# Gate and up projections of three feed-forward groups by seven half-size products instead of eight, in an encoder trunk on one core

## The chip, the cores and the metric

The kernel runs on one core of one Trainium2 chip. The metric is the device time of one execution in microseconds, as the median of several runs. The profile is one further execution, recorded by the hardware profiler; its span is counted from its first to its last instruction.

## The reference

The reference is a two-layer encoder trunk on 256 tokens of width 1024, all in float32. Cut to what matters here:

```python
def swiglu(h, w_gate, w_up, w_down):
    return (jax.nn.silu(h @ w_gate) * (h @ w_up)) @ w_down

for l in range(2):
    x = x + 0.5 * swiglu(rms_norm(x, ffn1_norm[l]), ffn1_w_gate[l], ffn1_w_up[l], ffn1_w_down[l])
    ...   # windowed attention with sinks, differential attention, one output projection
    x = x + 0.5 * swiglu(rms_norm(x, ffn2_norm[l]), ffn2_w_gate[l], ffn2_w_up[l], ffn2_w_down[l])
return rms_norm(x, final_norm)
```

So there are four feed-forward stages. In each, `w_gate` and `w_up` are 1024 x 2816 and `w_down` is 2816 x 1024.

## The kernel before

**Split products.** Every float32 weight tile is cut into a high and a low part. ScalarE (ACT) writes the high part (`whi`, a CAST of the loaded tile `raw`), VectorE (DVE) writes the rest (`wlo`, a TENSOR_TENSOR subtract of `raw` and `whi`). The normalised input x and the hidden values are cut in the same way, into two halves of a tile `s`. A product is then three TensorE (PE) matmuls: x high with w high, x low with w high, x high with w low. Tokens come in two tiles of 128, which are the stationary operand; the weights stream through as 512 columns.

**Steps.** One weight tile is a step: 128 partitions x 4 k-blocks x 512 columns, 1 MB. The SyncE queue (SP) loads it into one of 6 `raw` buffers, `emit_split` (line 167) cuts it in two halves of 128 x 1024 into one of 3 `whi` and one of 3 `wlo` buffers, and PE uses it in 24 matmuls (4 k-blocks, 2 token tiles, 3 matmuls each). A hidden group is 512 columns of gate and of up: four steps for gate and up (two k-halves each) and two steps for the down projection of the group before (`down`, line 623). The 2816 columns are groups 0 to 4 and a last half-wide one (lines 642 to 666). Between the first and the second gate step PE turns the hidden values of the group before with 8 transposes (`turn`, line 609), ACT and DVE cut the result into `hT`.

**What sets the order.** The order of every engine's queue is the order in which the program emits instructions (`keep_in_program_order`; inside the attention a scheduler may move them). `weights()` (line 219) returns the parts of the next step and first calls `ahead`, which emits the cut of the step after the next (`LOOK` is 2), a preparation step (`prep`) one step further, and the loads of up to 8 steps further while a `raw` buffer is free. Each queue works in order: an instruction that waits holds up all that is behind it. PSUM has 8 banks, 4 of which hold the down projection's sums through the whole stage.

**Code that lies idle.** The kernel already has `seven` (line 115), `make_sums` (line 304), `prod` (line 565) and `by_seven` (line 575). They are used for the groups named in `SEVEN` (line 31), which is empty, so that they never run. Also in the file and unchanged are `quarter` and `summed` (lines 333 and 340), which hand `prod` a quarter of x or one of the sums.

Of the kernel before, what the change touches and what calls it, by code (L numbers as in the profile page):

```python
# [27 lines left out]
LOOK, AHEAD = 2, 8  # L28
N_RAW, N_HI, N_LO = 6, 3, 3
N_S4 = 16  # L30
SEVEN = ()


@with_exitstack
def trunk(ctx: ExitStack, tc: tile.TileContext, x, n1, g1, u1, d1, nm, w_in, sink,
# [31 lines left out]
    def nm_(s):  # L67
        uid[0] += 1
        return f"{s}_{uid[0]}"

    def bank():
        return ps.tile([P, 512], F32, tag="ps", bufs=8, name=nm_("ps"))

    def halves(b):
        return b.rearrange("p (a n) -> p a n", a=2)

    def blk(dt=F32R):
        return s4.tile([P, 2, 512], dt, tag="s4", name=nm_("s4"))

    def tmp(tag="tmp", bufs=5, shape=(P, 2, 256), dt=F32):  # L80
        return tp.tile(list(shape), dt, tag=tag, bufs=bufs, name=nm_(tag))
# [137 lines left out]
    def weights(look=LOOK):  # L219
        i = at["use"]  # L220
        at["use"] += 1
        if i > 1:
            ahead(i + look)
        return loaded.pop(i)

    for l in range(DEPTH):
        def ffn_specs(wg, wu, wd):
# [3 lines left out]
            for g in range(1, NGRP):  # L231
                downs = [down(g - 1, h) for h in range(2)]
                if g in SEVEN:
                    specs.extend(seven(wg[l], wu[l], g * 512, downs))
# [38 lines left out]
    class Norm:  # L273
# [30 lines left out]
        def make_sums(self):  # L304

            self.sm = []

            def part(b, t):

                vs = [f(self.xs[2 * b + i]) for i in range(2)]  # L310
                return [[v[:, :, c + t * P:c + (t + 1) * P] for v in vs] for c in (0, S)]

            def make(x, y, op, rest):
                v = tmp().rearrange("p a (c s) -> p (a c) s", c=2)
                for i in range(2):
                    vi = v[:, 2 * i:2 * i + 2]
                    dve.tensor_tensor(vi, x[i], y[i], op=op)
                    for z, o in rest:
                        dve.tensor_tensor(vi, vi, z[i], op=o)
                sm = blk().rearrange("p a (c s) -> p (a c) s", c=2)  # L320
                act.copy(sm[:, :, 0:P], v)
                dve.tensor_tensor(sm[:, :, P:S], v, f(sm[:, :, 0:P]), op=ALU.subtract)
                self.sm.append(sm)
                return [v[:, 0:2], v[:, 2:4]]

            add, sub = ALU.add, ALU.subtract
            (t0h, t0l), (t1h, t1l), (b0h, b0l), (b1h, b1l) = [part(b, t) for b in range(2) for t in range(2)]
            s1 = make(b1h, t1h, sub, [(b1l, add), (t1l, sub)])
            s2 = make(s1, t0h, add, [(t0l, add)])
            make(t1h, t0h, sub, [(t1l, add), (t0l, sub)])  # L330
            make(b0h, s2, sub, [(b0l, add)])

        def quarter(self, t, b):

# [48 lines left out]
    norm = Norm(0)  # L383
# [86 lines left out]
    def tokens(accs, xs, w, k0, ks=range(4), first=0, last=KC - 1, order=None):  # L470

        hi, lo = w
        for k, t in (order or [(k, t) for k in ks for t in range(2)]):
            kk = k0 + k
            xv = xs[kk // 2][:, kk % 2]
            xh, xl = xv[:, t * P:(t + 1) * P], xv[:, S + t * P:S + (t + 1) * P]
            pe.matmul(accs[t], lhsT=xh, rhs=hi[:, k], start=kk == first, stop=False)
            pe.matmul(accs[t], lhsT=xl, rhs=hi[:, k], start=False, stop=False)
            pe.matmul(accs[t], lhsT=xh, rhs=lo[:, k], start=False, stop=kk == (last if isinstance(last, int) else last[t]))
# [63 lines left out]
    def ffn(norm, aside=None, before=None, final=False):  # L543
        def silu(out_, acc, t):
            act.activation(out_, acc, AF.Silu, scale=norm.r[:, t:t + 1])
            return out_

        def gate(gs):
            g = []
            for t in range(2):  # L550
                n = gs[t].shape[1]
                g.append(silu(tmp().rearrange("p a n -> p (a n)")[:, :n], gs[t], t))
            return g

        def up(h, acc, g, t):
            n = acc.shape[1]
            dve.scalar_tensor_tensor(h[:, t, :n], in0=acc, scalar=norm.hr[:, t:t + 1], in1=g, op0=ALU.mult, op1=ALU.mult)

        def hidden(g, us):
            h = blk(F32)  # L560
            for t in range(2):
                up(h, us[t], g[t], t)
            return h

        def prod(xo):
            hi, lo = weights()
            acc = bank()
            for k in range(4):
                xh, xl = xo(k)
                pe.matmul(acc, lhsT=xh, rhs=hi[:, k], start=k == 0, stop=False)  # L570
                pe.matmul(acc, lhsT=xl, rhs=hi[:, k], start=False, stop=False)
                pe.matmul(acc, lhsT=xh, rhs=lo[:, k], start=False, stop=k == 3)
            return acc

        def by_seven(h, g):

            flat = lambda: tmp().rearrange("p a n -> p (a n)")

            def put(o, x, y, op):
                dve.tensor_tensor(o, x, y, op=op)  # L580
                return o

            p1 = prod(norm.quarter(0, 0))
            m1 = flat()
            act.copy(m1, p1)
            p7 = prod(norm.summed(2))
            hT = turn(h, 2)
            p6 = prod(norm.summed(1))
            u2 = put(flat(), p6, m1, ALU.subtract)
            u3 = put(flat(), p7, u2, ALU.add)  # L590
            down(hT, g - 1, 0, weights())
            h = blk(F32)
            p2 = prod(norm.quarter(0, 1))
            g0 = put(m1, p2, m1, ALU.add)
            silu(g0, g0, 0)
            p4 = prod(norm.quarter(1, 1))
            g1 = put(flat(), p4, u3, ALU.subtract)
            silu(g1, g1, 1)
            p5 = prod(norm.summed(0))
            put(u3, u3, p5, ALU.subtract)  # L600
            put(u2, u2, p5, ALU.subtract)
            up(h, u3, g1, 1)
            p3 = prod(norm.summed(3))
            put(u2, u2, p3, ALU.add)
            up(h, u2, g0, 0)
            down(hT, g - 1, 1, weights())
            return h

        def turn(hs, n):
            out_ = []  # L610
            for i in range(n):
                sl = halves(bank())
                for c in range(2):
                    for t in range(2):
                        pe.transpose(sl[:, c, t * P:(t + 1) * P], hs[:, t, (2 * i + c) * P:(2 * i + c + 1) * P], ident)
                hb = blk()
                split(hb, sl)
                out_.append(hb)
            return out_

        accs = [[bank(), bank()] for _ in range(2)]

        def down(hT, g, h, w):
            tokens(accs[h], [None] * (2 * g) + hT, w, 4 * g, last=(FC - 1, G4 - 1) if final and h else FC - 1)


        gs, us = [bank(), bank()], [bank(), bank()]
        if before is None:
            before = norm.late
        before(0)  # L630
        ws = (weights(), weights(LOOK - 1))
        for k in (0, 2):
            if k:
                before(1)
            for sl, w in zip((gs, us), ws):
                tokens(sl, norm.xs, w, 0, (k, k + 1))
        before(2)
        tokens(gs, norm.xs, weights(), 4)
        g = gate(gs)
        tokens(us, norm.xs, weights(), 4)  # L640
        h = hidden(g, us)
        for n in range(1, NGRP):
            if n + 1 == min(SEVEN, default=0):
                norm.make_sums()
            if n == 3 and aside is not None:
                aside()
            if n in SEVEN:
                h = by_seven(h, n)
                continue
            gs = [bank(), bank()]  # L650
            tokens(gs, norm.xs, weights(), 0)
            hT = turn(h, 2)
            tokens(gs, norm.xs, weights(), 4)
            g = gate(gs)
            us = [bank(), bank()]
            for k0 in (0, 4):
                tokens(us, norm.xs, weights(), k0)
            h = hidden(g, us)
            for hh in range(2):
                down(hT, n - 1, hh, weights())  # L660

        gu = [bank(), bank()]
        tokens(gu, norm.xs, weights(), 0)
        hT = turn(h, 2)
        tokens(gu, norm.xs, weights(), 4)
        h = hidden(gate([b[:, 0:256] for b in gu]), [b[:, 256:512] for b in gu])
        return accs, hT, lambda: turn(h, 1)
# [278 lines left out]
    for l in range(DEPTH):  # L946
# [7 lines left out]
        if not final:  # L954
            norm = Norm((l + 1) * 8)
# [71 lines left out]
```

## Time and profile before

| what | value |
|---|---|
| median of 3 runs | 964.58 us (964.55 to 965.61) |
| the profiled execution, its own time | 964.2 us |
| its span | 962.4 us |
| TensorE clock granted, mean | 0.997 of full |
| PE busy | 951.3 us, 99% of the span |
| weight loads of PE (PEld) busy | 807.9 us, 84% |
| DVE busy | 557.4 us, 58% |
| ACT busy | 478.2 us, 50% |
| POOL busy | 20.1 us, 2% |
| read from HBM | 167.54 MB, 175 GB/s over the span |

Each engine is one row of the profile. Matmuls overlap each other, so the durations of single matmuls add up to more than the busy time, and the pitch between them has to be read from start times. A row of the timeline is start, time from the first start to the last end, engine, operation, output and inputs, count, and in brackets how long the engine had stood idle before and who ended that.

### The profile page before, as it was taken

The numbers are of one execution on the slowest core, as the hardware profiler recorded it, in microseconds if no ns is written. First come the engines' busy times: TensorE is split into PE (matmuls) and PEld (weight loads), VectorE is DVE, ScalarE is ACT, GpSimd is POOL, SyncE is SP. The second block draws the span as 40 slices with busy tenths as digits, with TensorE's granted clock in tenths as the row PEclk, the third lists the DMA queues.
The fourth block names the chain that finished last, engine by engine and source line by source line (L and its number), as shares of the span: only waits on it lengthen the run. The fifth ranks groups of instructions, "written<-read, shape, count | busy, mean of one in ns | idle before, by whom it ended". The sixth has DMA issues, their size and how long they took to land.

```text
span 962.4 us, 12393 instructions
## 1 busy us (share of the span) xinstructions
PE 951.3 (99%) x4940; PEld 807.9 (84%) x4940; DVE 557.4 (58%) x854; ACT 478.2 (50%) x781; POOL 20.1 (2%) x49
## 2 busy tenths in 40 slices
PE   8999999999999999999999999999999999999997
PEld 6888888899888888888888888888999888888886
DVE  5555545579756555545665445556796665445453
ACT  7544444467735543443554434435676464434443
POOL 0300000000000000000000000000000000000001
PEclk9999999999999999999999999999999999999998
DMA  9965555655425565555556555556551446565501
GB/s 338 329 218 175 177 187 204 176 176 132 132 91 173 188 205 179 192 188 185 174 180 210 179 185 198 183 176 179 172 174 47 161 150 214 175 227 189 175 1 44
DMA packets 98218, 169.39 MB, mean 176 GB/s; under 512 B 3182, under 2 KB 30896, under 8 KB 98160
## 3 DMA queue, kind: packets, MB, share of 16 engines
q1 hardware_dynamic: 96816, 167.27, 52.2%
q0 software_dynamic: 256, 0.29, 0.4%
q10 hardware_dynamic: 1088, 1.05, 0.3%
q8 instruction: 38, 0.62, 0.3%
q14 instruction: 20, 0.16, 0.0%
HBM read 167.54 MB, written 1.05 MB: 175 GB/s over the span
## 4 chain that ended last, share of the span: by engine, by line
PE 98%; DMA 0%; issue 0%; DVE 0%; ACT 0%; POOLq 0%; POOL 0%; ACTq 0%; DVEq 0%
PE ps L50 98%; DMA xk<-in_x_dram 0%; DVE s L50 0%; ACT tmp L50 0%; DVE xk L50 0%; POOLq L1022 0%; POOL rf L50 0%; ACTq L50 0%; DVE rf L50 0%; DVEq L50 0%
## 5 line engine op out<-in xcount | busy, mean ns | idle before, releaser
L50 PE MATMUL ps<-whi,s 128*128 128x512 f32 (+1 forms) x2316 | 717.5, 391 | 0.0
L50 DVE TENSOR_TENSOR wlo<-raw,whi 128x1024 fp32r<-128x1024 f32 (+2 forms) x392 | 378.6, 1014 | 237.7 <-ACT whi L50 234.7
L50 PEld LDWEIGHTS ps<-whi,s 128*128 128x128 f32 x2316 | 431.2, 188 | 87.2 <-ACT whi L50 0.3
L50 ACT CAST whi<-raw 128x1024 fp32r<-128x1024 f32 (+2 forms) x392 | 323.9, 884 | 264.0 <-PE ps L50 245.0
L50 PE MATMUL ps<-wlo,s 128*128 128x512 f32 x1158 | 450.2, 389 | 0.0
L50 PEld LDWEIGHTS ps<-wlo,s 128*128 128x128 f32 x1158 | 217.7, 188 | 45.4 <-DVE wlo L50 0.4
L50 PE MATMUL ps<-s,whi 128*128 128x256 f32 x448 | 82.7, 286 | 0.0
L50 ACT CAST s<-ps 128x512 fp32r<-128x512 f32 x48 | 26.0, 589 | 97.4 <-PE ps L50 97.4
L50 DVE TENSOR_TENSOR s<-ps,s 128x512 fp32r<-128x512 f32 x48 | 31.1, 687 | 72.9 <-ACT s L50 72.9
L50 PEld LDWEIGHTS ps<-s,whi 128*128 128x128 f32 x448 | 70.1, 192 | 1.1
L50 PE MATMUL ps<-s,wlo 128*128 128x256 f32 x224 | 63.3, 283 | 0.0
L50 ACT ACTIVATE tmp<-ps,r 128x512 f32<-128x512 f32 (+1 forms) x48 | 30.8, 654 | 46.9 <-PE ps L50 46.8
L50 DVE SCALAR_TENSOR_TENSOR s<-ps,hr,tmp 128x512 f32<-128x512 f32 (+1 forms) x48 | 32.4, 705 | 31.8 <-PE ps L50 25.4
L50 PEld LDWEIGHTS ps<-s,wlo 128*128 128x128 f32 x224 | 42.9, 192 | 0.0
L50 PE MATMUL ps<-ident,s 128*128 128x128 f32 x304 | 39.6, 273 | 0.0
L50 PEld LDWEIGHTS ps<-ident,s 128*128 128x128 f32 x304 | 35.1, 141 | 4.7
L50 ACT ACTIVATE s<-s,negm 128x256 f32<-128x256 f32 x64 | 31.9, 501 | 7.4 <-DVE negm L50 7.4
L50 ACT ACTIVATE s<-ps,gcol 128x256 fp32r<-128x256 f32 x48 | 19.3, 473 | 19.1 <-PE ps L50 19.0
L50 DVE SCALAR_TENSOR_TENSOR s<-ps,gcol,s 128x256 fp32r<-128x256 f32 x48 | 20.3, 477 | 12.5 <-ACT s L50 12.4
L50 POOL TENSOR_TENSOR r<-ms,mhalf 128x2 f32<-128x2 f32 x6 | 4.2, 707 | 629.9 <-DVE ms L50 629.9
L50 ACT ACTIVATE junk<-xk 128x512 f32<-128x512 f32 x24 | 15.3, 637 | 0.4
L50 PE MATMUL ps<-vA,s 128*128 128x64 f32 x128 | 14.7, 273 | 0.0
(93 smaller groups left out, 269.8 us busy)
## 6 DMA issues: line engine op xcount, KB each, us to landing
raw<-in_ffn_w_down_dram SPq DMA_DIRECT2D x44, 1024.0 KB, 4.9
raw<-in_ffn_w_gate_dram SPq DMA_DIRECT2D x39, 1024.0 KB, 5.0
raw<-in_ffn_w_up_dram SPq DMA_DIRECT2D x39, 1024.0 KB, 5.0
raw<-in_w_in_dram SPq DMA_DIRECT2D x14, 1024.0 KB, 5.1
raw<-in_ffn_w_gate_dram SPq DMA_DIRECT2D x8, 512.0 KB, 3.6
raw<-in_ffn_w_up_dram SPq DMA_DIRECT2D x8, 512.0 KB, 4.6
raw<-in_w_in_dram SPq DMA_DIRECT2D x8, 512.0 KB, 4.5
raw<-in_w_out_dram SPq DMA_DIRECT2D x4, 1024.0 KB, 4.8
```

The costliest lines, as they stand in the source:

```text
L50: ins = issue(*a, **k)
```

## The change

`SEVEN` becomes `(2, 3, 4)`. In these three groups of each of the four stages, gate and up are no longer four steps of 24 matmuls but seven products of 12 matmuls (Strassen's scheme in Winograd's form). The two token tiles are the rows, the two k-halves the inner dimension, gate and up the columns of a 2 x 2 block product. With a = gate, first k-half; b = up, first k-half; c = up, second k-half; d = gate, second k-half, the steps of one group are, in order:

| step | operand made by | matmuls |
|---|---|---|
| p1: a | load | 12 |
| p7: b + c | load of b, then a DMA of POOL that adds c into b's buffer | 12, then the 8 transposes |
| p6: a + b + c | DVE adds a into b's buffer (two instructions of 128 x 1024) | 12 |
| down, first half | load | 24 |
| p2: d | load | 12 |
| p4: d + (a + b + c) | DVE adds b's buffer into d's (two of 128 x 1024) | 12 |
| p5: a + b | a DMA of POOL that adds b (from HBM) into a's buffer | 12 |
| p3: c | load of c | 12 |
| down, second half | load | 24 |

Each of the nine steps is cut into `whi` and `wlo` like any other. The products are put together by seven DVE instructions of 128 x 512 (`put`), one ACT copy of p1, and the gate and up values follow by two ACT silu and two DVE instructions (`up`). Four sums of x (`make_sums`) are made once in each stage.

The diff also turns `make_sums` into a generator, one of whose four sums is made at each of four places in group 1, and takes the parts of the next step (`w = weights()`) ahead of the ACT copy and of the silu calls, so that the casts of a later step stand in front of these in ACT's queue.

```diff
-SEVEN = ()
+SEVEN = (2, 3, 4)
...
             s1 = make(b1h, t1h, sub, [(b1l, add), (t1l, sub)])
+            yield
             s2 = make(s1, t0h, add, [(t0l, add)])
+            yield
             make(t1h, t0h, sub, [(t1l, add), (t0l, sub)])
+            yield
             make(b0h, s2, sub, [(b0l, add)])
+            yield
...
-        def prod(xo):
-            hi, lo = weights()
+        def prod(xo, w):
+            hi, lo = w
...
-            p1 = prod(norm.quarter(0, 0))
+            p1 = prod(norm.quarter(0, 0), weights())
+            w = weights()
             m1 = flat()
             act.copy(m1, p1)
-            p7 = prod(norm.summed(2))
+            p7 = prod(norm.summed(2), w)
+            w = weights()
             hT = turn(h, 2)
-            p6 = prod(norm.summed(1))
+            p6 = prod(norm.summed(1), w)
...
-            p2 = prod(norm.quarter(0, 1))
+            p2 = prod(norm.quarter(0, 1), weights())
             g0 = put(m1, p2, m1, ALU.add)
+            w = weights()
             silu(g0, g0, 0)
-            p4 = prod(norm.quarter(1, 1))
+            p4 = prod(norm.quarter(1, 1), w)
             g1 = put(flat(), p4, u3, ALU.subtract)
+            w = weights()
             silu(g1, g1, 1)
-            p5 = prod(norm.summed(0))
+            p5 = prod(norm.summed(0), w)
             put(u3, u3, p5, ALU.subtract)
             put(u2, u2, p5, ALU.subtract)
+            w = weights()
             up(h, u3, g1, 1)
-            p3 = prod(norm.summed(3))
+            p3 = prod(norm.summed(3), w)
             put(u2, u2, p3, ALU.add)
+            w = weights()
             up(h, u2, g0, 0)
-            down(hT, g - 1, 1, weights())
+            down(hT, g - 1, 1, w)
...
-            if n + 1 == min(SEVEN, default=0):
-                norm.make_sums()
+            sums = norm.make_sums() if n + 1 == min(SEVEN, default=0) else iter(())
...
             g = gate(gs)
+            next(sums, None)
             us = [bank(), bank()]
             for k0 in (0, 4):
                 tokens(us, norm.xs, weights(), k0)
+                next(sums, None)
             h = hidden(g, us)
             for hh in range(2):
                 down(hT, n - 1, hh, weights())
+                if hh == 0:
+                    next(sums, None)
```

## Prediction

> **What bounds the kernel now.** I read the page's first part and its chain, then the timeline of one plain group by engine, then the grouped lines.
>
> ```profile
> PE 951.3 (99%) x4940; PEld 807.9 (84%) x4940; DVE 557.4 (58%) x854; ACT 478.2 (50%) x781; POOL 20.1 (2%) x49
> PE 98%; DMA 0%; issue 0%; DVE 0%; ACT 0%; POOLq 0%; POOL 0%; ACTq 0%; DVEq 0%
> ```
>
> PE is busy for 99% of the span and is 98% of the chain that ended last. Everything else is covered. So fewer matmuls are time gained, as long as DVE and ACT keep up in the groups concerned. What a matmul costs must be read from start times, since matmuls overlap. ACT's casts give a clean clock, because each waits for PE to leave a `whi` buffer:
>
> ```profile
> 115.07 2.01 ACT L50 CAST whi<-raw 128x1024 fp32r<-128x1024 f32 x2 [2.64 <-PE ps L50]
> 120.51 2.00 ACT L50 CAST whi<-raw 128x1024 fp32r<-128x1024 f32 x2 [3.43 <-PE ps L50]
> 125.95 2.01 ACT L50 CAST whi<-raw 128x1024 fp32r<-128x1024 f32 x2 [3.44 <-PE ps L50]
> ...
> 46.42 5.01 SPq L159 DMA_DIRECT2D raw<-in_ffn_w_down_dram  x2
> 79.97 5.01 SPq L159 DMA_DIRECT2D raw<-in_ffn_w_down_dram  x2
> ```
>
> The casts are 5.44 us apart: one step of 24 matmuls, 0.2267 us each. The two loads of the down weights come once in a group, so a plain group lasts 79.97 - 46.42 = 33.55 us. That is six steps (32.64) and the transposes:
>
> ```profile
> 103.33 1.03 PE L50 MATMUL ps<-ident,s 128*128 128x128 f32 x8
> 104.12 0.71 PE L50 MATMUL ps<-whi,s 128*128 128x512 f32 x2
> ```
>
> Eight transposes take 104.12 - 103.33 = 0.79 us; 32.64 + 0.79 = 33.4. Now DVE, in the same stage:
>
> ```profile
> 104.58 1.29 DVE L50 TENSOR_TENSOR s<-ps,s 128x512 fp32r<-128x512 f32 x2 [0.38 <-ACT s L50]
> ...
> 120.06 1.43 DVE L50 SCALAR_TENSOR_TENSOR s<-ps,hr,tmp 128x512 f32<-128x512 f32 x2 [1.54 <-PE ps L50]
> ...
> 132.48 2.36 DVE L50 TENSOR_TENSOR wlo<-raw,whi 128x1024 fp32r<-128x1024 f32 x2 [3.08 <-ACT whi L50]
> ...
> 214.59 2.77 DVE L50 TENSOR_TENSOR wlo<-raw,whi 128x256 fp32r<-128x256 f32 x8
> ...
> L50 DVE TENSOR_TENSOR wlo<-raw,whi 128x1024 fp32r<-128x1024 f32 x256 | 302.1, 1222 | 227.6 <-ACT whi L50 224.6
> L50 DVE TENSOR_TENSOR wlo<-raw,whi 128x256 fp32r<-128x256 f32 x32 | 11.1, 419 | 0.0
> L50 DVE TENSOR_TENSOR s<-ps,s 128x512 fp32r<-128x512 f32 x48 | 31.1, 687 | 72.9 <-ACT s L50 72.9
> L50 ACT CAST whi<-raw 128x1024 fp32r<-128x1024 f32 x256 | 256.4, 1052 | 240.6 <-PE ps L50 235.4 <-issue 5.1
> L50 ACT CAST s<-ps 128x512 fp32r<-128x512 f32 x48 | 26.0, 589 | 97.4 <-PE ps L50 97.4
> ```
>
> A pair lasts pitch plus one duration, so the pitch of 128x1024 on DVE is 2.36 - 1.22 = 1.14 us, of 128x512 1.29 - 0.69 = 0.60, of 128x256 (2.77 - 0.42) / 7 = 0.336. One cut of a step is 2.28 us of DVE and 2.01 of ACT. DVE stands idle 3.08 us before a cut, in every 5.44: that is the room into which the change puts its work.
>
> **What it removes.** Twelve matmuls in each of twelve groups (three in each of four stages): 144 x 0.2267 = 32.6 us of PE. A changed group needs 132 x 0.2267 + 0.79 = 30.7 us of PE.
>
> **What it adds on DVE.** A changed group has nine cuts (9 x 2.28 = 20.5), two additions of weights in two instructions each (4 x 1.14 = 4.6; same operands as the cut, SBUF to SBUF in float32), seven `put`, two `up` and two `hT` cuts (11 x 0.60 = 6.6): 31.7, and 0.1 more since the pair of `up` took 1.43: 31.8 us. A plain group has 6 x 2.28 + 2.6 = 16.3. So DVE goes from half the group to more than PE's 30.7. Even without one gap on DVE, a changed group lasts 31.8, and the gain is 33.5 - 31.8 = 1.7 a group, not 2.7. ACT stays below: nine cuts at 2.01, five or so at 0.6 to 0.7, 21.5 in all.
>
> **The gap.** DVE's queue in a changed group, from the built program's order: cut a, `up`, `put` of p3, cut b, add a to b, `up`, cut a+b+c, cut of the first down step, cut d, add to d, `hT` twice, `put` for u2 and u3, cut of d's sum, cut a+b, `put`, cut c, `put`, cut of the second down step, two `put`. Three `whi` buffers mean that the cast of a+b needs the buffer of the first down step, three steps earlier. And that step's second matmul needs the first `hT` cut, which stands behind cut d and the addition to d. Put as a walk from the end of p7 (T): PE does transposes and p6 and is at the down step at T + 3.5. ACT casts d from T (its buffer is p7's), DVE cuts it from T + 1.1 to T + 3.4, adds to d until T + 5.7, cuts `hT` until T + 6.4. PE, with one matmul done at T + 3.7, waits 2.7 us, more if DVE comes late to T, which a queue with 31.8 us of work does.
>
> The round closes so: from that `hT` cut PE does 23 matmuls (5.2), frees the buffer (0.2, an estimate from the cast at 115.07 against matmuls in pace), ACT casts the first half (1.05), DVE can cut a+b: 6.5 us. Meanwhile DVE has only the second `hT` cut, u2, u3 and the cut of d's sum: 4.1. All its other work, 31.8 - 4.1 = 27.7, lies in a row between the cut of a+b and the next `hT` cut. Period 27.7 + 6.5 = 34.2, and 0.2 for hand-offs between instructions that depend on each other (bounds 0 and 0.6): 34.4. Against 33.5 that is 0.9 more a group, 12 x 0.9 = 11 us. The 2.7 us saved on PE come back as some 3.7 us in which PE waits before the first down step.
>
> **The way in.** The four sums of x are 20 additions at 0.336 and four cuts at 0.60, 9.1 us of DVE in group 1, which has 33.5 - 16.3 = 17 free. Each also needs an ACT cast in between. Behind them stand, before the first p6: `up` 1.4, cut a 2.3, the fourth sum 2.5, cut b with half a cast 2.8, the addition 2.3; on ACT then a half cast 1.05, two casts of the down step 2.0 and the copy of p1 (0.59), because p6 takes p1's bank (four banks are held, the transposes take two). With the third sum (3.2) also late this is 18.2 from the end of the up product; PE needs 10.9 + 5.4 + 0.8 = 17.1. With hand-offs I take 2 us in each stage (bounds 0 and 4): 8. In the first stage the attention's constants stand in front of group 3 on DVE, four operations at 0.60 and small ones with a turn over ACT; covered before by the idle 3.08, not any more: 3 us (0 to 4.5). The casts in front of the silu cost nothing: g0 and g1 are needed steps later. Behind the last changed group DVE's load falls to half again, and it catches up: 0.
>
> **The adding DMAs.** Two a group from POOL's queue, whose other work does not stand beside them. None is in this trace.
>
> ```profile
> raw<-in_ffn_w_up_dram SPq DMA_DIRECT2D x39, 1024.0 KB, 5.0
> s<-in_lam_k_dram POOLq DMA_DIRECT2D x2, 64.0 KB, 7.8
> grow<-in_ffn_norm_dram POOLq DMA_DIRECT2D x1, 8.0 KB, 5.0
> ...
> 15.00:20.00 5.00, 5.00 (x24) 4.14 (x23) 5.00 (x11) 5.00 (x11) 0.00 (x0) 1.00 1.05 388
> ```
>
> A plain load of 1 MB lands in 5.0 us; the engines move 388 GB/s at most, so 2.7 us of that are bytes. POOL's own small DMAs took 5.0 to 7.8. How long there is: b's buffer falls free after the addition to d; its load takes 5.0, then c is added, and ACT must cast b 1.1 before DVE cuts it. In between DVE does `hT` twice, u2, u3 and the cut of d's sum (4.7), stands in the gap (6.5 - 4.1 = 2.4), then does four cuts and six instructions of 0.60 until cut b (12.7): 19.8, so 19.8 - 5.0 - 1.1 = 13.7 us are left for the adding DMA. For the one into a, from the addition to b to the cut of a+b, it is 15.7 by the same queue. Lower bound of its time 5.0 (nothing paid), upper bound 18.6: POOL's 7.8, three times the bytes (8.1), one load shared (2.7). I take 8 to 13, since most of POOL's 7.8 is fixed or queueing, hence nothing. At the upper bound the DMA for b is 4.9 late in each group: 59 us.
>
> The Trainium skill (Collectives: The Full Stack, The bandwidth ceiling) says an add in flight is slow since it needs two source reads, half the rate of a copy; no row here shows it. By it the estimate is two times the bytes, 7.8 + 5.4 = 13.2 us, just inside the 13.7, which is why late DMAs keep a large chance below.
>
> **The sum,** against the profiled execution's own 964.2 us (span 962.4; median of the runs 964.58, the same within 0.04%): 964.2 + 11 + 8 + 3 = 986. Its bounds: hand-offs at 0 and no way in, 964.2 + 8 = 972; all at the upper end, 964.2 + 16 + 16 + 4.5 = 1000.
>
> **Rivals.**
> - *DVE's order does no harm, faster.* If the `hT` cut came before the additions, or ACT freed DVE's waits, only the 31.8 would count: 964.2 - 12 x 1.7 + 0 to 8 of the way in = 944 to 952. Its point: the gap with hand-offs below 1.7 us a group. For it: DVE's idle 3.08 before each cut today. Against: the built order, and the 3-buffer ring that ties DVE to PE. Chance 0.13.
> - *The adding DMAs come late.* PE then waits for DVE, which waits for the cut of b. One us beyond 13.7 costs 12 us, so from one to 4.9 late: 998 to 1045. For it: two POOL-issued DMAs already took 7.8 at 64 KB. Chance 0.25.
> - *The clock falls.* TensorE's granted clock is 1.00 in the row above (the column before the last two), where PE never idles. If each of the twelve waits of 3.7 us brings as long a stretch at half clock, that is 12 x 1.85 = 22: 1008. The Trainium skill (TensorE: Matmul & The Clock Gate, What's actually happening) states such a fall to half after an idle window of about 3.4 us; no run here has shown it, and my waits lie at its edge. Chance 0.09.
> - *The change does nothing,* the waits eat exactly what is saved: 964. Chance 0.03.
>
> **The numbers.** The forecast of DVE's round, 986, has the remaining 0.50. A measurement of this kernel tells about 0.2% (2 us) from no change. Faster 0.13, same 0.03, slower 0.84. The range: DVE's case alone spans 972 to 1000. With a little below it for the prices (968), and up to 1040 for the falling clock and nearly all of the late DMAs, 968 to 1040 leaves out the faster rival and no change (0.16) and the worst of the DMAs (0.04).
>
> **What would show it.** Right: PE busy falls to some 94%, DVE rises to 75% or more; in the changed groups PE idles 3 to 4 us before the first matmuls with `hT`, released by DVE `s`, and the down loads of neighbouring changed groups stand 34 to 35 us apart; the first p6 of a stage waits some 2 us. Wrong: groups of 31 to 32 us; waits of ACT or DVE for DMA `raw` (then the DMAs bound it); PEclk below 9 in changed groups (then the clock).

## The result, and the profile after

The changed kernel takes 1001.5 us (median of four runs, 1000.4 to 1002.2), the kernel before 964.6 us. The ratio is 1.038 with a 95% interval of 1.036 to 1.040: slower by 37 us. The forecast was 986 (968 to 1040).

The page of the changed kernel, in the parts that answer to those shown of before (the first row is busy time by engine, the second the granted clock in tenths by slice, the third the chain that ended last by engine; the last row is a kind of DMA, with its size in KB and its median from issue to landing in us):

```profile
PE 940.9 (94%) x4796; PEld 792.5 (79%) x4796; DVE 779.1 (78%) x1154; ACT 563.8 (56%) x881; POOL 51.6 (5%) x73
PEclk9999898999999999999999999999999999998999
...
PE 71%; DVE 21%; issue 4%; ACT 2%; DMA 1%; SPq 0%; POOLq 0%; POOL 0%; ACTq 0%; DVEq 0%
...
raw<-in_ffn_w_up_dram POOLq DMA_DIRECT2D x24, 1024.0 KB, 8.4
```

PE fell from 99% busy to 94%, and DVE now holds 21% of the chain where it held none. The span grew by 36.2 us (998.6 against 962.4). PE's idle time grew from 962.4 - 951.3 = 11.1 to 998.6 - 940.9 = 57.7, so by 46.6. PE's busy time fell by 10.4 only, although 144 matmuls (32.6 us) are gone: 22.2 us of that came back in matmuls that last longer (most of it by the clock, as e2 shows). These are two losses, then, and the second one is not in the forecast's sum.

The first loss. What PE waits for (us in total, times, longest), and the queues of PE and DVE in a changed group of the second stage:

```profile
PE ps L50 <- DVE s L50: 38.0, 12, 3.6
PE ps L50 <- ACT tmp L50: 8.8, 5, 3.2
```

```profile
412.05 0.39 PE L50 MATMUL ps<-whi,s 128*128 128x512 f32 x1
415.53 0.50 PE L50 MATMUL ps<-whi,s 128*128 128x512 f32 x1 [3.10 <-DVE s L50]
```

```profile
405.70 6.91 DVE L50 TENSOR_TENSOR wlo<-raw,whi 128x1024 fp32r<-128x1024 f32 x6
412.51 2.37 DVE L50 TENSOR_TENSOR raw<-raw,raw 128x1024 f32<-128x1024 f32 x2
414.78 1.30 DVE L50 TENSOR_TENSOR s<-ps,s 128x512 fp32r<-128x512 f32 x2
415.98 1.43 DVE L50 TENSOR_TENSOR tmp<-ps,tmp 128x512 f32<-128x512 f32 x2
417.32 2.35 DVE L50 TENSOR_TENSOR wlo<-raw,whi 128x1024 fp32r<-128x1024 f32 x2
421.98 2.36 DVE L50 TENSOR_TENSOR wlo<-raw,whi 128x1024 fp32r<-128x1024 f32 x2 [2.31 <-ACT whi L50]
```

PE does one matmul of the down step at 412.05 and needs the first `hT` cut for the next; DVE is then at the last cuts of a row of three steps and at the addition to d (412.51). Only at 414.78 does it cut `hT`. Further down DVE itself stands idle for 2.31 us before the cut at 421.98, because ACT's cast waits for PE to leave a buffer. The twelve waits of PE come to 38.0 us. The additions to d appear as pieces of the chain that ended last, one for each changed group (start us, us):

```profile
378.39 2.27 DVE raw L50 x2
412.61 2.27 DVE raw L50 x2
446.82 2.27 DVE raw L50 x2
...
604.11 2.27 DVE raw L50 x2
639.97 2.27 DVE raw L50 x2
```

In the second stage the round is 34.2 us (412.61 - 378.39, 446.82 - 412.61). In the third it is 35.9 (639.97 - 604.11).

The second loss explains that difference. The same wait in the third stage, and what follows it (PE's rows, then columns of a window: PE, PEld, DVE, ACT and POOL busy, granted clock, DMA share, GB/s):

```profile
607.04 0.50 PE L50 MATMUL ps<-whi,s 128*128 128x512 f32 x1 [3.11 <-DVE s L50]
...
609.43 1.05 PE L50 MATMUL ps<-whi,s 128*128 128x512 f32 x2
610.29 0.63 PE L50 MATMUL ps<-wlo,s 128*128 128x512 f32 x1
610.71 1.06 PE L50 MATMUL ps<-whi,s 128*128 128x512 f32 x2
```

```profile
415.50:421.50 6.00, 5.97 (x26) 4.97 (x27) 4.13 (x5) 1.06 (x2) 0.75 (x1) 1.00 0.67 212
607.00:613.00 6.00, 5.96 (x19) 4.74 (x20) 4.14 (x5) 0.46 (x1) 0.00 (x0) 0.72 0.75 239
903.00:909.00 6.00, 5.98 (x14) 4.72 (x15) 4.12 (x5) 0.44 (x1) 0.87 (x1) 0.51 0.74 220
```

After the wait in the third stage three matmuls take 610.71 - 609.43 = 1.28 us, 0.427 each instead of 0.227, and in six microseconds 19 of them start where 26 did in the second stage. The granted clock is 0.72 there, and 0.51 in the last stage. Such a fall stands behind nine of the twelve waits; the three of the second stage have none. Over the nine windows of 6 us that begin where the waits end, the missing clock (1 less the granted clock) adds up to 3.02 windows, 3.02 x 6 = 18 us.

### The profile page after: what moved, and what is told of

The parts are those of the page before. It is cut to its first block, busy times and chain, and to the rows that moved or that the text cites. A ratio compares the mean times of both kernels' runs of the same rounds, so it can differ in the third digit from the quotient of the medians.

```text
span 998.6 us, 12675 instructions
## 1 busy us (share of the span) xinstructions
PE 940.9 (94%) x4796; PEld 792.5 (79%) x4796; DVE 779.1 (78%) x1154; ACT 563.8 (56%) x881; POOL 51.6 (5%) x73
## 4 chain that ended last, share of the span: by engine, by line
PE 71%; DVE 21%; issue 4%; ACT 2%; DMA 1%; SPq 0%; POOLq 0%; POOL 0%; ACTq 0%; DVEq 0%
PE ps L50 71%; DVE wlo L50 12%; DVE raw L50 4%; DVE tmp L50 2%; DVE s L50 2%; ACT whi L50 2%; DMA raw<-in_ffn_w_gate_dram 1%; ACT tmp L50 0%; DVE distA L50 0%; SPq L162 0%; DVE xk L50 0%; DVE distB L50 0%; ACT L50 0%; POOLq L1036 0%; POOL rf L50 0%
## 5 line engine op out<-in xcount | busy, mean ns | idle before, releaser
L50 PE MATMUL ps<-whi,s 128*128 128x512 f32 (+1 forms) x2220 | 704.4, 398 | 47.1 <-DVE s L50 38.0
L50 DVE TENSOR_TENSOR wlo<-raw,whi 128x1024 fp32r<-128x1024 f32 (+2 forms) x464 | 461.1, 1047 | 103.3 <-ACT whi L50 102.1
L50 PEld LDWEIGHTS ps<-whi,s 128*128 128x128 f32 x2220 | 421.3, 192 | 140.2 <-DVE s L50 43.3
L50 ACT CAST whi<-raw 128x1024 fp32r<-128x1024 f32 (+2 forms) x464 | 396.5, 908 | 238.9 <-PE ps L50 133.6
L50 PE MATMUL ps<-wlo,s 128*128 128x512 f32 (+1 forms) x1110 | 438.2, 395 | 0.0
L50 DVE TENSOR_TENSOR raw<-raw,raw 128x1024 f32<-128x1024 f32 x48 | 56.6, 1224 | 0.0
L50 POOL DMA_DIRECT2D raw<-in_ffn_w_up_dram x24 | 31.1, 1295 | 447.2 <-ACT whi L50 265.7
L50 ACT CAST s<-tmp 128x512 fp32r<-128x512 f32 (+1 forms) x22 | 13.2, 602 | 49.1 <-DVE tmp L50 49.1
L50 PEld LDWEIGHTS ps<-ident,s 128*128 128x128 f32 x304 | 35.1, 141 | 4.7
L50 ACT ACTIVATE s<-s,negm 128x256 f32<-128x256 f32 x64 | 31.8, 500 | 7.4 <-DVE negm L50 7.4
L50 DVE TENSOR_TENSOR tmp<-ps,tmp 128x512 f32<-128x512 f32 x48 | 33.1, 689 | 0.4
L50 ACT ACTIVATE s<-ps,gcol 128x256 fp32r<-128x256 f32 x48 | 19.2, 473 | 19.2 <-PE ps L50 19.1
L50 ACT ACTIVATE tmp<-ps,r 128x512 f32<-128x512 f32 (+1 forms) x24 | 14.4, 617 | 21.2 <-PE ps L50 21.2
```

What stands on the lines that cost most here:

```text
L50: ins = issue(*a, **k)
```

## The experiments

The theory was that two things make the loss: the place of the `hT` cut in DVE's queue, and the clock that falls behind the waits. The rivals were the adding DMAs, and DVE's mere sum of work.

**e1: the `hT` cut first.**

```
             p7 = prod(norm.summed(2), w)
-            w = weights()
             hT = turn(h, 2)
+            w = weights()
```

> The two `hT` cuts are emitted ahead of the cut of d and the addition to d; nothing else moves. Theory A (DVE's order makes PE wait 3.1 to 4.1 us before each first down step, and these waits bring the clock down): the twelve waits go, DVE's 31.8 us of work per group remain, PE waits some 2 us per group elsewhere, the granted clock returns to 0.99 or more, 958 to 972 us. Rival B (the adding DMAs are what is late): 1001 as before. Rival C (DVE's sum alone sets the round of 34.2 us, whatever its order): only the clock's part can go, 980 to 1001.

The line moved is part of the change itself: the diff takes `w = weights()`, and with it the cut of d and the addition to d, ahead of `turn`, where the idle code had `turn` first.

It took 983.9 us (977.6 to 989.3 in four runs), ratio 1.018 (1.013 to 1.023). 17.6 us are gone, but the time is far above what theory A expected, and the clock stays at 0.981 to 0.989 where 0.99 or more was expected. The time lies in rival C's range; the chain shows another cause. What ACT waits for, and two pieces of the chain:

```profile
ACT whi L50 <- DMA raw<-in_ffn_w_up_dram: 50.0, 7, 9.4
```

```profile
374.99 5.18 DMA raw<-in_ffn_w_up_dram
380.73 15.06 DMA raw<-in_ffn_w_up_dram
```

The waits before the first down step are gone. ACT now waits 50.0 us for weights in seven places, for b, which is loaded and then has c added by a DMA, here 15.06 us long. The forecast's rival of late DMAs, which does not occur in the changed kernel, occurs as soon as the first loss is repaired.

**e2: PE kept busy.** The twelve matmuls of p6 are run once more ahead of p6; the products are the same. 12 x 0.2267 = 2.7 us of work go where PE waited 3.1.

```
+            for k in range(fill):
+                xh, xl = xo(k)
+                pe.matmul(acc, lhsT=xh, rhs=hi[:, k], start=True, stop=False)
...
-            p6 = prod(norm.summed(1), w)
+            p6 = prod(norm.summed(1), w, 4)
```

> Before p6 PE runs p6's twelve matmuls once more into the same bank, 2.72 us of work in each changed group, overwritten by p6. DVE's and ACT's queues are those of the changed kernel. Theory A with the clock as a part of its own: the wait before the first down step shrinks from 3.1 or more to 0.5 or less, DVE's round stays at 34.2, the granted clock is 0.99 or more, and the time falls by the some 22 us that PE's matmuls were stretched, to 977 to 984 us, although PE does 144 matmuls more. If the clock does not depend on these waits: 1001 with a clock of 0.977, or more than 1001 if the fill comes on top (up to 1034).

984.0 us (983.6 to 984.3), ratio 1.020 (1.019 to 1.022). A kernel with 144 more matmuls is 17.5 us faster. Its page, what PE waits for, and the additions to d in two stages:

```profile
PE 956.9 (97%) x4940; PEld 807.5 (82%) x4940; DVE 779.1 (79%) x1154; ACT 562.9 (57%) x881; POOL 51.0 (5%) x73
PEclk9999999999999999999999999999999999999999
```

```profile
PE ps L50 <- DVE s L50: 5.3, 12, 0.9
```

```profile
371.73 2.27 DVE raw L50 x2
405.97 2.28 DVE raw L50 x2
...
596.12 2.27 DVE raw L50 x2
630.33 2.27 DVE raw L50 x2
```

The round is 34.2 us in both stages now, so DVE's order still sets it; what went is the lowered clock. That is the size of the second loss: 17.5 us by the time, 18 by the windows, and 16.6 by PE's busy time (956.9 less the 32.6 of the additional matmuls is 924.3, against 940.9 in the changed kernel). The remaining 5.6 of the 22.2 above are there without a lowered clock, too.

**e3: no adding DMAs.** c is not added into b, nor b into a.

```
-                pool.dma_start(raws[to], w[k], accum_op=ALU.add)
+                pass
```

> Leaves out the two adding DMAs of each changed group (b + c and a + b are then not formed); all else as in the changed kernel. Theory A: 24 DMAs that landed in 8.4 us (median) were in time, so 997 to 1004 us. Rival B: the time falls by 10 us or more.

1003.3 us in one run. As far as one run can tell, the adding DMAs cost nothing in the changed kernel.

**e4: no additions to d.** DVE loses 24 instructions of 1.14 us; d is cut without a and b in it.

```
-                Step(**n, prep=plus(b, d), src=d, free=[b, d]),
+                Step(**n, src=d, free=[b, d]),
```

> Leaves out the two DVE additions of the weights' sum to d in each changed group (p4 then has d alone). 2.28 us less DVE work per group, all of it ahead of the `hT` cuts. Theory A: the wait before the first down step falls to 1.0 to 1.4 us, the clock stays up, the round falls to 32 us: 950 to 962 us. Rival B: 1001. Rival C: the round falls by 2.3 as well, 12 x 2.3 = 27 and the clock only if the waits get short: 952 to 974.

969.7 us in one run, 32 less than the changed kernel, with the clock undisturbed. It stays above what theory A expected and lies in rival C's range; the same row as in e1 says by what:

```profile
ACT whi L50 <- DMA raw<-in_ffn_w_up_dram: 25.6, 8, 7.0
```

27 us of DVE work bring 32. The clock's part goes with the waits, and late DMAs eat some of what is gained; how much of each was not separated.

**e6: both moves, three groups.** In e1, PE also waited 23.6 us for ACT's `tmp`, the copy of p1 whose bank p6 takes. Here the copy stands ahead of the casts of the next step as well.

```
-            w = weights()
             m1 = flat()
             act.copy(m1, p1)
+            w = weights()
             p7 = prod(norm.summed(2), w)
-            w = weights()
             hT = turn(h, 2)
+            w = weights()
```

> The same two moves (hT ahead of the cut of d, the copy of p1 ahead of the weights) with all three groups by seven products, as in the change. The wait of p6 for the copy, 1.4 to 1.7 us in most groups of e1, should go. Theory A (DVE's sum of work sets the round, 31.8 us): 983.9 less some 12 x 1.5 = 966, 960 to 970. Rival B (the adding DMAs, 13 to 15 us in e1, set the round): the wait moves to them and the time stays at 975 to 986.

982.8 us (982.1 to 982.9), ratio 1.019 (1.017 to 1.021), the rival's range. A round of the chain that ended last, and SP's queue beside it:

```profile
373.12 2.28 DVE raw L50 x2
...
375.41 4.96 DMA raw<-in_ffn_w_up_dram
...
380.94 13.57 DMA raw<-in_ffn_w_up_dram
...
394.61 1.05 ACT whi L50
...
395.69 2.36 DVE wlo L50 x2
...
408.98 2.29 DVE raw L50 x2
...
411.29 5.21 DMA raw<-in_ffn_w_up_dram
```

```profile
381.28 0.37 SPq L159 DMA_DIRECT2D raw<-in_ffn_w_gate_dram  x1
384.15 0.37 SPq L159 DMA_DIRECT2D raw<-in_ffn_w_up_dram  x1
387.02 0.37 SPq L159 DMA_DIRECT2D raw<-in_ffn_w_down_dram  x1
```

Addition to d, load of b, adding DMA, cast, cut, and so on to the next addition to d: 408.98 - 373.12 = 35.9 us. While the adding DMA is on its way (380.94 to 394.51) SP issues three more loads of 1 MB.

**e9: e6 without the adding DMAs** (the edit of e3; the same additions are left out).

> The kernel of e6 (three groups by seven, hT first, copy first) without the two adding DMAs a group: c is not added into b nor b into a, all else is as it was. In the changed kernel leaving them out moved the time by less than 0.3%. Theory B (in e6 each group is one chain: additions on DVE, a load of b of 5.0 us, the adding DMA of 13.4 to 14, a cast, cuts, 36.0 in all; without it DVE's sum of 31.8 or PE's 30.7 sets the group): 982.8 - 12 x (36.0 - 31.8) = 932 and up to 20 more for the first groups of each stage, 935 to 955, no wait of ACT for DMA raw. Theory A (DVE's sum and the small waits before the transposes set the 36.0, the DMA only fills them): 972 to 984.

947.3 us (946.6 to 948.1), ratio 0.982 (0.980 to 0.983): 35.5 us below e6, as theory B had it. The first matmul with `hT`, in neighbouring changed groups:

```profile
391.86 0.50 PE L50 MATMUL ps<-whi,s 128*128 128x512 f32 x1 [0.70 <-DVE s L50]
...
423.67 0.50 PE L50 MATMUL ps<-whi,s 128*128 128x512 f32 x1 [0.69 <-DVE s L50]
```

31.8 us: DVE's sum of work, the figure that the prediction worked out for a DVE without a gap. The same DMAs cost nothing in e3 and 35.5 us here.

**e10, e11, e5: two groups of three.** Groups 2 and 4 alone go by seven products, with a plain group between them; PE saves 96 matmuls, 21.8 us. e10 is the changed kernel otherwise, e11 has hT's cut first as in e1, and e5 both moves as in e6.

```
-SEVEN = (2, 3, 4)
+SEVEN = (2, 4)
```

> The changed kernel with only groups 2 and 4 by seven products, its order left as the change has it. PE saves 22 us. Theory A (the order of DVE's queue makes PE wait some 3.1 us before the first down step of each changed group, whether or not a plain group follows, and 2 us on the way in; some of these waits bring the clock down): before less 22, plus 8 x (3.1 + 2) = 41 at most, plus up to 8 x 1.5 for the clock: 975 to 995, PE waiting for DVE s 8 times before the down step. Rival C (the plain group between is what helped e5, the two moves do nothing): as e5, 943 to 950.

> The kernel of e10 (groups 2 and 4 by seven) with hT's cut ahead of the cut of d, the copy of p1 left where the change has it. Theory A (the waits of 2.4 to 3.1 before the first down step, 22 us in e10, and the clock's fall behind them, some 17, come from hT alone; the copy's waits of 1.4 stay): e5 plus 4 to 8 x 1.4, 950 to 958, clock above 0.99. Rival (both moves are needed, the wait for the copy is long enough to bring the clock down): 960 to 975.

> The changed kernel with three edits: the cut of hT ahead of the cut of d, the copy of p1 into m1 ahead of the second set of weights, and only groups 2 and 4 by seven products, so that a plain group stands between them. PE saves 8 x 2.72 = 22 us instead of 33. Theory A (DVE's load and order set the round, the plain group has 33.5 - 16.3 = 17 us of DVE free in which it catches up): what is left is the 1.1 us by which DVE's 31.8 exceeds PE's 30.7 in each of 8 groups, and 0 to 4 us of way in a stage pair, 964.6 - 22 + 9 + 0 to 6 = 945 to 958, clock 0.99 or more. Rival B (with hT ahead the adding DMAs are late and bind every changed group, 1.6 us or more in each as the excess over the forecast was in e1): 8 x 1.6 = 13 more, 960 to 972, with waits of ACT for DMA raw in both changed groups of a stage.

e10 took 987.9 us (ratio 1.022, 1.019 to 1.025), e11 949.7 (0.985, 0.983 to 0.986), e5 945.4 (0.980, 0.979 to 0.982). What PE waits for in e10, one of its waits, and the window behind it:

```profile
PE ps L50 <- DVE s L50: 22.0, 8, 3.1
```

```profile
149.24 0.50 PE L50 MATMUL ps<-whi,s 128*128 128x512 f32 x1 [2.37 <-DVE s L50]
```

```profile
149.20:155.20 6.00, 5.96 (x19) 4.74 (x20) 4.14 (x5) 0.47 (x1) 0.00 (x0) 0.72 0.71 192
```

The place of the `hT` cuts is worth 38.3 us (e10 to e11): 22.0 of waits and, by PE's busy time (946.9 against 931.3 for the same matmuls), 15.6 of clock. DVE's sum of work is the same in both (busy 719.9 and 718.9), so rival C, for which only the sum counts, falls here. All eight waits of e10 bring a fall, those of 2.4 us too. The copy is worth 4.2 more (e11 to e5). The plain group by itself is worth little: with PE's saving in full the time would be 964.6 - 32.6 = 932.0 with three groups and 964.6 - 21.8 = 942.8 with two; against that the changed kernel loses 5.8 us in each changed group and e10 5.6. But e6 against e5 shows that the moves need it: the two are 37 us apart, with fewer products by seven in the faster one. In e5 PE is busy 99% again and runs through a changed group without a stop (page; one piece of the chain from 371.96 on):

```profile
PE 930.5 (99%) x4844; PEld 789.5 (84%) x4844; DVE 718.9 (76%) x1086; ACT 538.3 (57%) x853; POOL 40.6 (4%) x65
```

```profile
371.96 38.08 PE ps L50 x172
```

e5 is the fastest kernel of this study, 2.0% faster than before and 5.6% than the changed one.

**e7 and e12: the casts where they were.** Each product takes its weights when it starts, as before the change; `hT` and the copy come first then, too. e7 has three groups, e12 two.

```
-        def prod(xo, w):
-            hi, lo = w
+        def prod(xo):
+            hi, lo = weights()
```

> The changed kernel with the order of casts in by_seven as it was before the change: each product takes its weights when it starts, behind silu and the additions. Theory A (as predicted, the casts ahead of silu cost and bring nothing, because g0 and g1 are needed steps later): 998 to 1004. Rival (the casts ahead are what lets DVE start its cuts without standing idle, and DVE is the engine that sets the round, so an ACT step of about 1 us more per group in DVE's row costs 12 us): 1008 to 1018.

> The kernel of e7 (each product takes its weights when it starts, which puts the casts behind silu, the copy and hT's cut, as before the change) with groups 2 and 4 by seven. Against e5 only the casts behind silu and behind the additions differ. Theory A (the casts ahead save some 8 us in 12 groups, as e7 against e6): e5 plus 8 x 0.7 to 8 x 1.9, 951 to 962. Rival (with a plain group between there is slack, and the casts' place costs nothing): 944 to 949.

e7 took 990.7 us (989.9 to 992.5), below both expectations, which had overlooked that this order also puts the `hT` cut first and so takes the clock's part away (mean granted clock 0.995, against 0.977 in the changed kernel). Compared with e6, it is 7.9 us slower; the two differ in whether the casts and cuts of later steps stand ahead of the two silu and of `up`, or behind them. e12 took 961.1 (960.9 to 961.4), 15.6 more than e5. ACT's queue in e12, then in e5, around the two silu:

```profile
372.89 0.73 ACT L50 ACTIVATE tmp<-tmp,r 128x512 f32<-128x512 f32 x1 [3.51 <-DVE tmp L50]
373.52 1.98 ACT L50 CAST whi<-raw 128x1024 fp32r<-128x1024 f32 x2
```

```profile
368.74 0.72 ACT L50 ACTIVATE tmp<-tmp,r 128x512 f32<-128x512 f32 x1 [1.50 <-DVE tmp L50]
369.37 1.99 ACT L50 CAST whi<-raw 128x1024 fp32r<-128x1024 f32 x2
```

With the casts behind it, a silu that waits 3.51 us for its sum holds up the casts of a step that needs nothing from it. In e12 DVE then stands idle for 1.73 us before each of the two cuts behind the silu, in e5 not at all. The earlier place is worth 8 us in twelve groups (where e6 is bound by its late DMAs) and 16 in eight. What the place behind `up` has in this by itself no run shows.

**e8: the sums of x at once,** ahead of group 1's first gate step.

```
-            sums = norm.make_sums() if n + 1 == min(SEVEN, default=0) else iter(())
+            sums = iter(())
+            if n + 1 == min(SEVEN, default=0):
+                for _ in norm.make_sums():
+                    pass
```

> The changed kernel with the four sums of x made all at once ahead of the first gate step of group 1, as before the change. 9.1 us of DVE and their casts on ACT then stand in one row in each of 4 stages. Theory A (DVE has 17 us free in group 1 and PE runs at most one cut ahead, so one row of 9.1 makes PE wait by what exceeds DVE's free 3.08 before a cut, but in exchange the fourth sum is out of the way of the first changed group): 0 to 2.5 us a stage, 1000 to 1011. Rival (the way in costs nothing either way): 1000 to 1002.

1007.4 us (1006.0 to 1011.1), ratio 1.045 (1.043 to 1.047). Taking the sums one by one is worth some 6 us, 1.5 a stage.

## Why the prediction was right in its direction and short in its size

**What PE saves:** right. In e5, where nothing else is late, the time fell by 19.2 of 21.8.

**DVE's order and round:** right. The wait before the second matmul of the down step was forecast at 3 to 4 us and is 3.1 to 3.6. The gap on DVE was forecast at 2.4 and is 2.31. The round was 34.4 and is 34.2 wherever the clock holds. DVE's sum without a gap, 31.8, is what e9 shows. Undoing the order removes the waits (e1, e11).

**The way in, and the attention's constants:** right as a sum. Without the clock's part (e2) the loss is 984.0 - 964.6 = 19.4 us; 12 x (34.2 - 33.5) = 8.4 of that are rounds, which leaves 11.0 where 8 + 3 were forecast. The even sum is in part luck. In e2 the additions to d of the first stage, where the attention's constants stand, are 38.2 and 35.1 us apart instead of 34.2, which is 4.9 more where 3 were forecast; 6.1 then remain for the four ways in, where 8 were. PE's waits for ACT `tmp` say the same: four of 1.4 us, one in each stage, and a fifth of 3.2 in the first stage.

**The adding DMAs:** right for this kernel, at nothing (e3), with a median of 8.4 us inside the estimate of 8 to 13. How the estimate was made up was wrong, and two errors offset each other. From 442.0 to 444.0 us of the changed kernel's trace only packets of one adding DMA, issued at 439.88, are moved: the DMA engines are busy in full (share 1.00) and carry 158 GB/s, where plain loads reach 388. So the bytes cost more than twice what a plain load's do. What stands ahead of them is short: until 441.4, 1.5 us from the issue, nothing moves, while the prediction took most of 7.8 us as fixed or queueing. The Trainium skill (Collectives: The Full Stack, The bandwidth ceiling) tells of a reduce-scatter between cores that its add needs two source reads and so runs at half the rate of a copy; the trace agrees for this add into a tile (158 against 388 GB/s). The 13.2 us that the prediction worked out with that rule are too long for an add by itself because of the 7.8, and near the 13.2 to 14.4 of the adds into b in e6, where three other loads are under way. The prediction's room of 13.7 us for b explains both results. In the changed kernel DVE's gap of 2.4 and two `hT` cuts of 0.6 were contained in it. With the order undone those 3.6 go, and 10.1 are left for 13.6: 3.5 us late, against rounds that are 35.9 - 31.8 = 4.1 longer. The wait that the change brought was the cover of its DMAs.

**The casts ahead of silu:** forecast at nothing, since g0 and g1 are needed steps later. That looked at who needs silu and not at what stands behind it on ACT. With the cuts ahead of `up` they bring 8 to 16 us (e7, e12). This is a gain of the change, so the forecast, which took the changed order as it was, does not suffer by it.

**The clock:** here the sum is wrong. The term "the clock falls" was priced well, 12 x 1.85 = 22 us, against 17.5 (e2); nine falls of about 2.0 instead of twelve of 1.85. But it stood as a rival with a chance of 0.09, and the forecast's sum has nothing for it. It is no rival to DVE's round: it comes on top of it, since it is made by the same waits. 986 + 17.5 = 1003.5, against 1001.5 measured. The row from which the prediction argued (clock 1.00 where PE never idles) said nothing about waits of 3 us, and the bounds of 972 to 1000 should have carried the term in full. The measured time is beyond these bounds; it lies inside the range because that had been stretched to 1040 for the clock and the late DMAs. The sign that the prediction named for the clock (PEclk below 9 in changed groups) appeared together with its signs of DVE's round.

**The two rivals of the other side** fell for this kernel, and hold for others: e9 is "only the 31.8 counts" (947.3, forecast 944 to 952), and e6 is "the DMAs come late". Either needs the `hT` cut first.

## What to carry to other kernels

When work moves from PE to an engine that is half idle, write out that engine's queue in order over a whole round, and look for the small instruction on which PE waits behind a row of large ones: here two cuts of 0.6 us in the wrong place cost 38 us in eight groups, and placing them well was free. A wait can be the cover of a slow transfer, so work out again how much room each transfer has once the wait is gone. And leave the newly loaded engine a plain stretch in which to catch up: two groups by seven gain 19 us where three with the same order lose 18.

## What the runs showed of the hardware

- The clock fell behind waits shorter than I had thought: behind all eight of 2.37 to 3.14 us in e10, behind nine of twelve of 3.1 to 3.6 in the changed kernel, and not behind the three of its second stage, which are as long, nor behind the one of 3.2 us for ACT `tmp` in its first stage. The Trainium skill (TensorE: Matmul & The Clock Gate, What's actually happening) tells of an idle window of 3.4 us that runs freely; by these rows 2.37 us of waiting can be enough. That the place of the wait in a window decides between a fall and none would fit the rows, but no run here moved a wait to show it.
- Work done in vain can pay: 144 additional matmuls in e2 made the kernel 17.5 us faster.
- A DMA that adds 1 MB from memory into a tile took 13.2 to 14.4 us where plain loads of 1 MB were issued beside it (e6; three of them in the round shown), a plain load of 1 MB right ahead of it some 5 us. By itself it filled the DMA engines at 158 GB/s, against 388 for plain loads.
